# Six modulation chunks of the scan stage: products summed over row blocks on VectorE

## The chip, the core and the metric

The kernel runs on one core of one Trainium2 chip. The metric is the device time of one execution in microseconds; three runs of the kernel before gave 2157.26, 2160.35 and 2162.36 us, with a median of 2160.35 us. TensorE (PE) multiplies matrices into PSUM, VectorE (DVE) and ScalarE (ACT) work on vectors, GpSimd (POOL) does elementwise work and issues some DMAs, SyncE (SP) issues the other DMAs from one queue, in order. Each engine takes its instructions in a fixed order, and a wait at the head of an engine holds what stands behind it.

## The reference

Two layers of a diffusion trunk on 512 latent tokens and 256 context tokens of width 1024. Layer 0 mixes by a bidirectional state-space scan, layer 1 by neighbourhood attention, and both end with an MLP. Every layer is modulated by a linear map of the conditioning vectors:

```
c_act, c_ctx_act = silu(c), silu(c_ctx)
m_lat = split(c_act     @ mod_w[i] + mod_b[i], 6)   # per layer i: shift, scale, gate, twice
m_ctx = split(c_ctx_act @ mod_w[i] + mod_b[i], 6)
h = rmsnorm(x, g[0]) * (1 + m[1]) + m[0]
proj = h @ w_in                                     # then the scan, chunks of 128 tokens
scores = (C_i . B_j) * exp(cum_i - cum_j) * dt_j
y = scores @ x + exp(cum) * (C @ state)
```

The product with `mod_w` (1024 rows, 6144 columns for a layer) has only two vectors on its other side, so it is a matter of reading weights.

## The kernel before

Activations stand with channels on the partitions and tokens on the free axis. Every weight block of 128x1024 is loaded by SyncE (`wload`), split by ScalarE into a high part `wh` (L118) and by VectorE into the rest `wl` (L119), and multiplied in three products (`mm3`, L143).

The state-space stage is a loop over four groups `g`. A group has eight units (`conv_unit`): each projects one block of 128 channels (48 products of 512 or 256 columns in L143), convolves it over three tokens (one pass of ScalarE in L611, four on VectorE in L613 and L614) and passes it through silu. Groups 2 and 3 have four gate units (`z_unit`) in their middle, and eight more follow. `scan(g, ...)` is a generator; the scan of a group is stepped, `step(1)` behind pairs of products of a unit, while the units of the next group run. So scan and projection share every engine. Of a scan, VectorE makes: a mask product G (L645), and for each of 12 halves of chunks the minimum of E with cum (L713), the product of E with G (L718) and the sum of both directions (L719); then the state parts (L674 to L678), the products eb (L764) and the sum into y (L766). GpSimd weighs tokens (L662) and adds the terms (L768). TensorE multiplies E (L746), the states (L762) and the weighted tokens (L667), and needs the finished E for the first of these.

Between units one step of a further generator runs, `pieces`: the modulation of layer 0, chunks 4 to 9, each a block of 1024x512 weights loaded in four quarters `mraw` of 128x1024. One quarter holds four row blocks of 256 columns. The load of the next quarter is put into a list (`later`), which a unit issues behind its fourth pair of rows (`flush`). There is one buffer for `mraw`.

`mod_pieces` makes the products on TensorE: for each row block, 32 columns of `cact` (the two conditioning vectors stand in the first two of them) against 256 columns of weights, four row blocks in four column groups of the array (`mod_unit`, L169). `mod_finish` copies the result on ScalarE (L184), transposes it four times (L186), and VectorE sums the four row blocks (L190) and adds the bias (L191). `mod_sums`, which the MLP of layer 0 uses already, does the weighted sum over the row blocks first, then a sum over partitions with ones (L251), one copy (L255), two transposes (L257) and the bias (L262).

The order on each engine is set by a scheduler from the order in the code, the dependences and its own durations; `tc.high_priority()` moves a few instructions ahead.

Of the kernel before, what the change touches and what calls it, by code (L numbers as in the profile page):

```python
# [50 lines left out]
def trunk(ctx: ExitStack, tc: tile.TileContext, a, out, dbg=None, stop=None):  # L51
    nc = tc.nc
    pe, act, dve, pool, sp = nc.tensor, nc.scalar, nc.vector, nc.gpsimd, nc.sync
# [25 lines left out]
    def sps(tag="s"):  # L79
        return psums[tag].tile([P, 512], F32, tag=tag, name=tag)  # L80
# [83 lines left out]
    def mod_unit(ps, q, raw):  # L164


        hf, kg = divmod(q, 2)
        for j in range(4):
            mm = pe.matmul(ps[32 * j:32 * j + 32, hf * 256:hf * 256 + 256], lhsT=cact[:, 8 * kg + 2 * j:8 * kg + 2 * j + 32],  # L169
                      rhs=raw[:, j * 256:j * 256 + 256], start=kg == 0, stop=kg == 1)  # L170
        return mm.ins

    def mod_finish(l, ch, ps, cp, row_pool=None):

        for hf in range(2):
            if row_pool:
                row = row_pool.tile([P, 256], F32, tag="row", name="row", bufs=2)
            else:
                row = small.tile([P, 256], F32, tag="rt", name="row", bufs=1)
            if row_pool:  # L180
                with tc.high_priority():
                    dve.tensor_copy(row, ps[:, hf * 256:(hf + 1) * 256])
            else:
                act.activation(row, ps[:, hf * 256:(hf + 1) * 256], AF.Copy)  # L184
            for b in range(2):
                pe.transpose(cp[:, (2 * hf + b) * P:(2 * hf + b + 1) * P], row[:, b * P:(b + 1) * P], ident)  # L186
        bias = mb[:, l, ch * 4:(ch + 1) * 4].unsqueeze(2).broadcast_to([P, 4, 2])
        mt = small.tile([P, 4, 2], F32, tag="modt", name="modt", bufs=2)
        with tc.high_priority():
            dve.tensor_reduce(mt, cp.rearrange("p (b j s) -> p b s j", b=4, j=4)[:, :, 0:2], AX.X, ALU.add)  # L190
            dve.tensor_tensor(modc[:, l, ch * 4:(ch + 1) * 4, :], mt, bias, ALU.add)  # L191
# [7 lines left out]
    def mod_pieces(chunks, pool_, later=None):  # L199

        def load(l, ch, q):
            raw = pool_.tile([P, 1024], F32, tag="mraw", name="mraw", bufs=1)
            if later is None:
                sp.dma_start(raw, a["modw"][l, ch, q])
            else:
                later.append((raw, a["modw"][l, ch, q]))
            return raw

        todo = [(l, ch, q) for l, ch in chunks for q in range(4)]
        raw = load(*todo[0])  # L210
        yield
        for i, (l, ch, q) in enumerate(todo):
            if q == 0:
                ps = sps()
            mod_unit(ps, q, raw)
            if i + 1 < len(todo):
                raw = load(*todo[i + 1])
            if q == 3:
                mod_finish(l, ch, ps, sps())
            yield  # L220

    def mod_sums(chunks, pool_):

        def load(l, ch, q):
            raw = pool_.tile([P, 1024], F32, tag="mraw", name="mraw", bufs=1)
            sp.dma_start(raw, a["modw"][l, ch, q])
            return raw

        todo = [(l, ch, q) for l, ch in chunks for q in range(4)]
        raw = load(*todo[0])  # L230
        yield
        for i, (l, ch, q) in enumerate(todo):
            hf, kg = divmod(q, 2)
            if kg == 0:
                ms = pool_.tile([P, 2, 256], F32, tag="msum", name="msum", bufs=1)
            for j in range(4):
                for s in range(2):
                    c = cact[:, 8 * kg + 2 * j + s:8 * kg + 2 * j + s + 1]
                    w, t = raw[:, j * 256:(j + 1) * 256], ms[:, s]
                    if kg == 0 and j == 0:  # L240
                        act.activation(t, w, AF.Copy, scale=c)
                    else:
                        dve.scalar_tensor_tensor(t, w, c, t, ALU.mult, ALU.add)
            if i + 1 < len(todo):
                raw = load(*todo[i + 1])
            if q == 1:
                ps = sps()
            if kg == 1:
                for s in range(2):
                    j = 2 * hf + s  # L250
                    pe.matmul(ps[32 * j:32 * j + 32, :256], lhsT=ones[:, :32], rhs=ms[:, s], start=True, stop=True)  # L251
            if q == 3:
                cp = sps()
                row = small.tile([P, 256], F32, tag="rt", name="row", bufs=1)
                act.activation(row, ps[:, :256], AF.Copy)  # L255
                for b in range(2):
                    pe.transpose(cp[:, b * P:(b + 1) * P], row[:, b * P:(b + 1) * P], ident)  # L257
                bias = mb[:, l, ch * 4:(ch + 1) * 4].rearrange("p (h b) -> p h b", h=2)
                to = modc[:, l, ch * 4:(ch + 1) * 4, :].rearrange("p (h b) s -> p h b s", h=2)
                got = cp[:, :256].rearrange("p (b h s r) -> p h b s r", b=2, h=2, s=2)  # L260
                for h in range(2):
                    dve.tensor_tensor(to[:, h], got[:, h, :, :, 0], bias[:, h].unsqueeze(2).broadcast_to([P, 2, 2]), ALU.add)  # L262
            yield
# [172 lines left out]
    with tc.tile_pool(name="p0", bufs=1) as p0:  # L436
# [6 lines left out]
        for ch in (0, 2, 1, 3):  # L443
            for pr in range(2):
                raw = p0.tile([P, 2, 1024], F32, tag="raw0", name="raw0", bufs=8)
# [58 lines left out]
    ssd = sstack.enter_context(tc.tile_pool(name="ssd", bufs=1))  # L504
# [82 lines left out]
    later = []  # L587
# [219 lines left out]
            if pending is not None and next(pending, 0) == 0:  # L807
                pending = None

    pieces = mod_pieces([(0, ch) for ch in range(4, 10)], ssd, later)  # L810
    nz = 0
    for g in range(GROUPS):
        B, C, X = [None] * 2, [None] * 2, [None] * 4
# [597 lines left out]
```

## Time and profile before

| | before |
|---|---|
| median of three runs | 2160.35 us |
| profiled execution | 2166.39 us, span 2164.6 us |
| TensorE busy | 2060.4 us (95%) |
| VectorE busy | 1379.0 us (64%) |
| ScalarE busy | 1022.6 us (47%) |
| GpSimd busy | 445.1 us (21%) |
| mean granted clock of TensorE | 0.978 |

The shares are means over stages. The stage of the change goes from about 55 us to 376 us: the first load of a quarter is issued at 54.9 us, the last at 359.5 us. A busy TensorE is not TensorE at its peak, since the ends of its records are modelled; costs are read here from the start of one group of products to the start of the next. Line numbers are those of the kernel before; in the changed kernel those behind L226 are 3 higher.

### The profile page before, as it was taken

The numbers are of one execution on the slowest core, as the hardware profiler recorded it, in microseconds if no ns is written. First come the engines' busy times: TensorE is split into PE (matmuls) and PEld (weight loads), VectorE is DVE, ScalarE is ACT, GpSimd is POOL, SyncE is SP. The second block draws the span as 40 slices with busy tenths as digits, with TensorE's granted clock in tenths as the row PEclk, the third lists the DMA queues.
The fourth block names the chain that finished last, engine by engine and source line by source line (L and its number), as shares of the span: only waits on it lengthen the run. The fifth ranks groups of instructions, "written<-read, shape, count | busy, mean of one in ns | idle before, by whom it ended". The sixth has DMA issues, their size and how long they took to land.

```text
span 2164.6 us, 32307 instructions
## 1 busy us (share of the span) xinstructions
PE 2060.4 (95%) x12588; PEld 1731.3 (80%) x12588; DVE 1379.0 (64%) x2351; ACT 1022.6 (47%) x1781; POOL 445.1 (21%) x438
## 2 busy tenths in 40 slices
PE   6999998999999899999999999889999889999996
PEld 3787876878878767888888888678898768889896
DVE  5657967577683778657667244488777774345355
ACT  4575756567472644323223123456556643323244
POOL 0005435146361340000000002513222230000002
PEclk8999999999999899999999999999999999999998
DMA  6456748357575522333333121321111124222233
GB/s 256 129 162 184 242 148 240 119 165 219 194 223 178 207 78 78 114 128 119 120 114 117 59 67 60 108 79 50 57 54 54 50 80 135 90 96 89 97 108 117
DMA packets 93868, 269.70 MB, mean 125 GB/s; under 512 B 13074, under 2 KB 21652, under 8 KB 93716
## 3 DMA queue, kind: packets, MB, share of 16 engines
q1 hardware_dynamic: 85268, 242.47, 34.1%
q0 software_dynamic: 8448, 25.18, 4.4%
q8 instruction: 99, 1.62, 0.3%
q14 instruction: 53, 0.43, 0.1%
HBM read 244.27 MB, written 23.33 MB: 124 GB/s over the span
## 4 chain that ended last, share of the span: by engine, by line
PE 62%; DVE 7%; ACT 3%; DMA 2%; issue 1%; POOL 1%; SPq 0%; DVEq 0%; ACTq 0%; POOLq 0%
PE acc L943 21%; PE acc L995 20%; PE acc L143 8%; PE a L1090 4%; PE a L1101 2%; PE yp L1176 1%; DVE wl L119 1%; PE pt L1161 1%; ACT wh L118 1%; DVE xa L398 1%; PE s L251 1%; DVE ya L397 1%; PE sc L1146 1%; PE sc L1147 1%; PE s L306 0%
## 5 line engine op out<-in xcount | busy, mean ns | idle before, releaser
L118 ACT ACTIVATE wh<-raw 128x1024 fp32r<-128x1024 f32 (+1 forms) x241 | 254.3, 1056 | 648.5 <-PE acc L995 225.8
L119 DVE TENSOR_TENSOR wl<-raw,wh 128x1024 fp32r<-128x1024 f32 (+1 forms) x241 | 298.0, 1237 | 212.0 <-ACT wh L118 208.5
L143 PE MATMUL acc<-hh,wh 128*128 128x512 f32 (+1 forms) x976 | 288.1, 372 | 6.6 <-ACT wh L118 2.6
L143 PE MATMUL acc<-hl,wh 128*128 128x512 f32 (+1 forms) x976 | 266.3, 348 | 0.5 <-DVE hl L800 0.5
L143 PE MATMUL acc<-hh,wl 128*128 128x512 f32 (+1 forms) x976 | 264.7, 347 | 2.0 <-DVE wl L119 2.0
L995 PE MATMUL acc<-ah,wh 128*128 128x512 f32 (+1 forms) x832 | 246.7, 346 | 4.5 <-DVE ya L1001 4.4
L943 PE MATMUL acc<-hh,wh 128*128 128x258 f32 (+2 forms) x1024 | 240.7, 315 | 5.9 <-ACT hh L415 5.2
L995 PE MATMUL acc<-ah,wl 128*128 128x512 f32 (+1 forms) x832 | 245.0, 345 | 0.8 <-DVE wl L119 0.8
L995 PE MATMUL acc<-al,wh 128*128 128x512 f32 (+1 forms) x832 | 244.9, 344 | 0.0
L943 PE MATMUL acc<-hl,wh 128*128 128x258 f32 (+2 forms) x1024 | 239.8, 313 | 1.0 <-DVE hl L416 0.9
L943 PE MATMUL acc<-hh,wl 128*128 128x258 f32 (+2 forms) x1024 | 240.5, 313 | 0.1
L143 PEld LDWEIGHTS acc<-hh,wh 128*128 128x128 f32 (+1 forms) x976 | 156.3, 191 | 60.2 <-issue 38.1
L943 PEld LDWEIGHTS acc<-hh,wh 128*128 128x128 f32 x1024 | 160.6, 191 | 25.3 <-issue 6.6
L143 PEld LDWEIGHTS acc<-hh,wl 128*128 128x128 f32 (+1 forms) x976 | 155.2, 192 | 27.7 <-DVE wl L119 2.5
L143 PEld LDWEIGHTS acc<-hl,wh 128*128 128x128 f32 (+1 forms) x976 | 155.8, 192 | 25.2 <-issue 1.0
L943 PEld LDWEIGHTS acc<-hh,wl 128*128 128x128 f32 x1024 | 161.3, 191 | 14.0 <-issue 1.6
L943 PEld LDWEIGHTS acc<-hl,wh 128*128 128x128 f32 x1024 | 160.2, 190 | 14.4 <-DVE hl L416 2.4
L352 POOL TENSOR_TENSOR syy<-syy,last 128x512 f32<-128x512 f32 (+2 forms) x24 | 39.3, 1638 | 613.5 <-ACT last L342 613.5
L995 PEld LDWEIGHTS acc<-ah,wh 128*128 128x128 f32 x832 | 139.4, 189 | 29.8 <-issue 8.6
L995 PEld LDWEIGHTS acc<-ah,wl 128*128 128x128 f32 x832 | 139.6, 189 | 22.5 <-issue 1.2
L995 PEld LDWEIGHTS acc<-al,wh 128*128 128x128 f32 x832 | 139.7, 189 | 20.6 <-issue 0.4
L1001 DVE TENSOR_TENSOR ya<-ya,acc 128x768 f32<-128x768 f32 (+2 forms) x56 | 40.6, 726 | 163.5 <-PE acc L995 163.3
(327 smaller groups left out, 3849.5 us busy)
## 6 DMA issues: line engine op xcount, KB each, us to landing
raw<-in_w_dram SPq DMA_DIRECT2D x136, 512.0 KB, 3.3
mraw<-in_modw_dram SPq DMA_DIRECT2D x72, 512.0 KB, 3.4
raw<-in_win_dram SPq DMA_DIRECT2D x48, 512.0 KB, 4.5
E<-crow SPq DMA_DIRECT2D x96, 256.0 KB, 5.0
eb<-erow POOLq DMA_DIRECT2D x96, 128.0 KB, 5.5
raw<-in_wout_dram SPq DMA_DIRECT2D x24, 512.0 KB, 3.5
raw<-in_modw_dram SPq DMA_DIRECT2D x8, 1024.0 KB, 17.3
raw<-in_wqk_dram SPq DMA_DIRECT2D x16, 512.0 KB, 3.3
```

Of the source, the lines that this page charges most:

```text
L118: act.activation(wh[:, :n], raw[:, :n], AF.Copy)
L119: dve.tensor_tensor(wl[:, :n], raw[:, :n], wh[:, :n].bitcast(F32), ALU.subtract)
L143: mm = pe.matmul(acc[:m, s0:s1], lhsT=ww[:, i * m:(i + 1) * m], rhs=xx[:, k, s0:s1], start=first and i == 0 and j == 0, stop=last and i == ...
L251: pe.matmul(ps[32 * j:32 * j + 32, :256], lhsT=ones[:, :32], rhs=ms[:, s], start=True, stop=True)
L352: (dve if i == 1 and s1 - s0 == 256 else pool).tensor_tensor(t[:, s0:s1], t[:, s0:s1], d, ALU.add)
L397: dve.tensor_tensor(y[:, k, sl], y[:, k, sl], R, ALU.mult)
L398: dve.tensor_tensor(x[:, k, sl], x[:, k, sl], y[:, k, sl], ALU.add)
L943: pe.matmul(acc[:, d0:d0 + s1 - s0], lhsT=ww[wi], rhs=xx[:, k, s0:s1], start=k == 0 and j == 0, stop=k == KB - 1 and j == 2)
L995: pe.matmul(acc[:, s0:s1], lhsT=ww[:, k * P:(k + 1) * P], rhs=xx[:, s0:s1], start=k == 0 and j == 0, stop=k == KB - 1 and j == 2)
L1001: dve.tensor_tensor(y, y, acc[:, p0:p1], ALU.add)
L1090: pe.matmul(acc[:, :s1 - s0], lhsT=ws[ww][:, k * P:(k + 1) * P], rhs=xx[:, k, s0:s1], start=k == 0 and j == 0, stop=k == KB - 1 and j == 2)
L1101: pe.matmul(acc, lhsT=xx[:, k, i * P:(i + 1) * P], rhs=w[ww][:, sl], start=k == 0 and n == 0, stop=k == KB - 1 and n == 2)
```

## The change

The six chunks that run beside the state-space stage are made by `mod_sums` in place of `mod_pieces`. For that `mod_sums` learns to put its loads into the list `later`.

```
-    def mod_sums(chunks, pool_):
+    def mod_sums(chunks, pool_, later=None):
 
         def load(l, ch, q):
             raw = pool_.tile([P, 1024], F32, tag="mraw", name="mraw", bufs=1)
-            sp.dma_start(raw, a["modw"][l, ch, q])
+            if later is None:
+                sp.dma_start(raw, a["modw"][l, ch, q])
+            else:
+                later.append((raw, a["modw"][l, ch, q]))
             return raw
...
-    pieces = mod_pieces([(0, ch) for ch in range(4, 10)], ssd, later)
+    pieces = mod_sums([(0, ch) for ch in range(4, 10)], ssd, later)
```

What `mod_sums` does with a quarter (unchanged by the diff):

```
            for j in range(4):
                for s in range(2):
                    c = cact[:, 8 * kg + 2 * j + s:8 * kg + 2 * j + s + 1]
                    w, t = raw[:, j * 256:(j + 1) * 256], ms[:, s]
                    if kg == 0 and j == 0:
                        act.activation(t, w, AF.Copy, scale=c)
                    else:
                        dve.scalar_tensor_tensor(t, w, c, t, ALU.mult, ALU.add)
```

So a chunk has 28 such instructions on VectorE and 4 on ScalarE, and on TensorE 4 sums with ones in place of 16 products, and 2 transposes in place of 4.

VectorE in the scan of group 0, around the weight split for the unit that follows the first X block (L613, L614 and, 3 higher, L616, L617 are the convolution; sf the forward state). Before:

```order
L718 TENSOR_TENSOR E<-E,G 128x1024
L614 SCALAR_TENSOR_TENSOR xT<-acc,cols,xT 128x511
L613 SCALAR_TENSOR_TENSOR xT<-acc,cols,xT 128x255
L719 TENSOR_TENSOR E<-E 128x512
L614 SCALAR_TENSOR_TENSOR xT<-acc,cols,xT 128x255
L713 TENSOR_TENSOR E<-E,cum 128x1024
L764 TENSOR_TENSOR eb<-eb,s 128x512 x2
L766 TENSOR_TENSOR y<-y,s 128x512
L677 TENSOR_TENSOR sf<-sf,dec 128x512
L713 TENSOR_TENSOR E<-E,cum 128x1024
L678 TENSOR_TENSOR sf<-sf,s 128x512
L119 TENSOR_TENSOR wl<-raw,wh 128x1024
```

The same place on VectorE with the change (E's minimum is L716, its product L721, its sum L722 there):

```order
L722 TENSOR_TENSOR E<-E 128x512
L617 SCALAR_TENSOR_TENSOR xT<-acc,cols,xT 128x511
L616 SCALAR_TENSOR_TENSOR xT<-acc,cols,xT 128x255
L246 SCALAR_TENSOR_TENSOR msum<-mraw,cact,msum 128x256
L617 SCALAR_TENSOR_TENSOR xT<-acc,cols,xT 128x255
L246 SCALAR_TENSOR_TENSOR msum<-mraw,cact,msum 128x256
L119 TENSOR_TENSOR wl<-raw,wh 128x1024
L246 SCALAR_TENSOR_TENSOR msum<-mraw,cact,msum 128x256 x6
L716 TENSOR_TENSOR E<-E,cum 128x1024 x2
L265 TENSOR_TENSOR modc<-s,cols 128x4 x2
L769 TENSOR_TENSOR y<-y,s 128x512
L680 TENSOR_TENSOR sf<-sf,dec 128x512
```

Eight additions of one quarter stand around the weight split, and two minima, a sum into y and the state step of the scan now stand behind them.

TensorE at the end of the third chunk, in the same scan. Before, with two transposes at a time and products with E between them:

```order
L143 MATMUL acc<-hl,wh 128x512
L186 MATMUL s<-consts,row 128x128 x2
L746 MATMUL s<-E,xtok 64x128 x4
L143 MATMUL acc<-hl,wh 128x256
L143 MATMUL acc<-hh,wl 128x512
L186 MATMUL s<-consts,row 128x128 x2
L143 MATMUL acc<-hh,wl 128x256
```

With the change (ones-products are L254, transposes L260, products with E L749):

```order
L254 MATMUL s<-msum,ones 32x256
L143 MATMUL acc<-hl,wh 128x256
L143 MATMUL acc<-hh,wl 128x512
L254 MATMUL s<-msum,ones 32x256
L143 MATMUL acc<-hh,wl 128x256
L143 MATMUL acc<-hh,wh 128x512
L143 MATMUL acc<-hh,wh 128x256
L143 MATMUL acc<-hl,wh 128x512
L260 MATMUL s<-consts,row 128x128 x2
L749 MATMUL s<-E,xtok 64x128 x8
```

The products with ones depend on VectorE's additions; four projection products behind the second of them come the transposes, which depend on ScalarE's copy, and then eight products with E.

## Rows read from the trace of the kernel before

**Rows 1.** Busy us and instructions of each engine by stretch, clock, DMA share, GB/s.
```profile
core 0: us, PE busy (x) PEld busy (x) DVE busy (x) ACT busy (x) POOL busy (x), PEclk, DMA share, GB/s
55.00:193.70 138.70, 136.17 (x822) 107.83 (x820) 85.74 (x138) 78.19 (x125) 21.34 (x25) 0.99 0.47 142
193.70:264.60 70.90, 67.84 (x466) 54.98 (x465) 65.12 (x82) 50.26 (x105) 40.16 (x42) 1.00 0.82 247
264.60:300.40 35.80, 35.21 (x210) 27.06 (x209) 20.98 (x31) 19.10 (x32) 8.16 (x7) 1.00 0.34 113
300.40:376.40 76.00, 70.34 (x447) 54.08 (x445) 59.73 (x64) 50.70 (x104) 42.33 (x43) 0.96 0.80 239
```

**Rows 2.** Waits from 55 to 380: waiter, releaser, us in total, times, longest.
```profile
DVE E L713 <- DMA E<-crow: 23.0, 12, 9.0
...
PE s L746 <- DVE E L719: 3.9, 4, 1.4
PE s L186 <- ACT row L184: 3.5, 2, 2.9
...
PE s L667 <- DVE y L766: 3.1, 1, 3.1
```

**Rows 3.** TensorE's timeline, old modulation products and transposes: start, us, instructions.
```profile
207.03 0.64 PE L169 MATMUL s<-mraw,cact 128*32 128x256 f32 x8
207.60 0.62 PE L143 MATMUL acc<-hh,wh 128*128 128x512 f32 x2
...
213.20 0.38 PE L186 MATMUL s<-consts,row 128*128 128x128 f32 x2
213.34 0.36 PE L143 MATMUL acc<-hh,wl 128*128 128x256 f32 x1
```

**Rows 4.** TensorE's timeline in the MLP, sums with ones, a pair and one alone.
```profile
858.42 0.77 PE L251 MATMUL s<-msum,ones 128*32 128x256 f32 x4
859.12 0.38 PE L943 MATMUL acc<-hh,wl 128*128 128x258 f32 x1
...
876.23 0.62 PE L251 MATMUL s<-msum,ones 128*32 128x256 f32 x2
876.78 0.39 PE L943 MATMUL acc<-hh,wl 128*128 128x258 f32 x1
```

**Rows 5.** VectorE's timeline in the MLP, three scaled additions and what follows.
```profile
863.72 1.27 DVE L243 SCALAR_TENSOR_TENSOR msum<-mraw,cact,msum 128x256 f32<-128x256 f32 x3
864.91 0.95 DVE L981 TENSOR_TENSOR al<-last,ah 128x768 fp32r<-128x768 f32 x1
```

**Rows 6.** Groups of ScalarE in the MLP: count, busy us, mean ns, idle before.
```profile
L241 ACT ACTIVATE msum<-mraw,cact 128x256 f32<-128x256 f32 x40 | 18.3, 499 | 11.9 <-DMA mraw<-in_modw_dram 11.8
```

**Rows 7.** VectorE's timeline at the end of the first scan, work ahead.
```profile
244.33 7.80 DVE L713 TENSOR_TENSOR E<-E,cum 128x1024 f32<-128x1024 f32 x4
...
256.26 1.23 DVE L718 TENSOR_TENSOR E<-E,G 128x1024 f32<-128x1024 f32 x1
257.52 0.69 DVE L719 TENSOR_TENSOR E<-E 128x512 f32<-128x512 f32 x1
```

**Rows 8.** Three lines of VectorE, 150 to 380: ns min/median/max, first and last start.
```profile
L718 DVE TENSOR_TENSOR E<-E,G x21: 1210/1224/2353, 151.5 to 368.3; 128x1024 f32<-128x1024 f32 x21
...
L719 DVE TENSOR_TENSOR E<-E x23: 677/685/1532, 150.0 to 371.0; 128x512 f32<-128x512 f32 x23
...
L764 DVE TENSOR_TENSOR eb<-eb,s x18: 674/680/689, 185.8 to 366.5; 128x512 f32<-128x512 f32 x18
```

**Rows 9.** VectorE's group of E's product in the first scan, 193.7 to 264.6.
```profile
L718 DVE TENSOR_TENSOR E<-E,G 128x1024 f32<-128x1024 f32 x9 | 12.3, 1364 | 1.3 <-ACT E L717 1.2
```

**Rows 10.** TensorE's timeline, a product of the scan that waited for PSUM.
```profile
336.68 2.04 PE L667 MATMUL s<-xw,btok 128*128 128x512 f32 x2 [3.10 <-DVE y L766]
```

**Rows 11.** The two stretches around this wait, columns as in rows 1.
```profile
335.00:340.00 5.00, 3.32 (x7) 2.12 (x8) 4.11 (x5) 3.76 (x11) 3.00 (x2) 0.57 0.62 203
340.00:345.00 5.00, 5.00 (x28) 3.89 (x27) 5.00 (x6) 0.00 (x0) 4.64 (x3) 0.75 0.28 97
```

## The prediction

> **What bounds the kernel now.** I read the slices of the page first, then sums of the stretch that the change touches, then the waits inside it, and last the timelines of TensorE and VectorE. In the stretches of the state-space stage [rows 1] TensorE is busy nearly all the time: 67.84 of 70.9 us between 193.7 and 264.6, where the scan of group 0 runs beside the projections of group 1, and 70.34 of 76.0 us between 300.4 and 376.4, where the scan of group 1 runs beside those of group 2. VectorE stands close behind it there: 65.12 of 70.9 us and 59.73 of 76.0 us. Before the first scan (55 to 193.7) it is busy for 85.74 of 138.7 us, and between the two scans (264.6 to 300.4) for 20.98 of 35.8 us. So TensorE bounds the stage as a whole, and in the scans VectorE is the second limit, with 5.8 and 16.3 us to spare. What TensorE waits for [rows 2] is small and of two kinds: E, which VectorE ends (3.9 us), and the end of a modulation chunk (3.5 us for the copy on ScalarE), and once, for 3.1 us, a PSUM tile that VectorE still had to read.
>
> **The change part by part.** It concerns six chunks of modulation, each of four loads: 24 steps, from about 55 us to 376 us.
>
> Removed on TensorE: 24 product steps. Such a step (four products of 32 columns, side by side in the array) runs from 207.03 to 207.60 [rows 3], so 0.57 us, 13.7 us in all. Six of twelve pairs of transposes go, 0.14 us each by the next two rows of the same group, 0.8 us.
>
> Added on TensorE: 12 pairs of sums with ones. The pair costs 0.70 us where its two stand together and 0.55 us for each where other work stands between them [rows 4]. In the changed order 5 pairs stand together and 7 apart: 3.5 + 7.7 = 11.2 us. TensorE is left with 13.7 + 0.8 - 11.2 = 3.3 us less work. The gain is small because the old products already shared the array four at a time.
>
> Added on VectorE: 28 scaled additions of 128x256 for a chunk, 168 in all. In the later stage that already works this way three of them take from 863.72 to 864.91 [rows 5], 0.397 us each, so 66.7 us. Their number by place, counted in the changed order between the same weight splits: 70 before 193.7, 34 in the first scan, 23 between the scans, 33 in the second, 8 after. The small reductions and additions at the end of a chunk, on both sides under half a microsecond each, are left out.
>
> Added on ScalarE: 24 scaled copies at 499 ns [rows 6], 12.0 us, less six row copies. It is idle for 20 us or more in each scan [rows 1], so I take nothing; without that cover it would be 2.5 us for each scan (five copies).
>
> What of the 66.7 us is hidden:
> - Before 193.7: 70 x 0.397 = 27.8 us into 53 us of idle time. Hidden but for delays of the softplus chain; 0 to 4 us, taken as 0.
> - First scan: 34 x 0.397 = 13.5 us into 5.8 us. In the old order VectorE works ahead here for the next scan [rows 7]: four minima in 7.80 us, and two products with their sums of 1.23 + 0.69 us. In the new order one minimum (1.95 us) and these two pairs (3.8 us) come after the stretch, so 5.8 us leave it. Work is 65.1 + 13.5 - 5.8 = 72.8 us in a stretch of 70.9. With no idle time left at all that is +1.9; with all of the old idle time still there (it comes from waits in order, not from lack of work), 72.8 + 5.8 = 78.6, +7.7. I take +5, since the idle time of before was nearly all spent on waits that stay.
> - Between the scans: 23 x 0.397 = 9.1 us and the 5.8 us put off make 14.9 us, against 14.8 us idle. 0 to 6 us, taken as +2.
> - Second scan: 33 x 0.397 = 13.1 us into 16.3 us idle. Over the whole stage VectorE's wait for E to land is 23.0 us [rows 2]; part of the 16.3 us is such waits, behind which an addition can stand only if the fixed order has one there. 0 (all fit) to 13.1 (none); taken as +3.
> - After 376.4: 8 additions, VectorE idle for longer than that, nothing.
>
> New waits: TensorE now waits for the sums of VectorE before the ones-products, and for one row copy before the transposes; in the third chunk the 8 products with E of the scan stand right behind these transposes. Half as many row copies speaks for less than the old 3.5 us, the lagging sums for more; from -3.5 (gone) to +6 (each of 12 pairs waits half a microsecond), taken as 0. The load of the next quarter waits for the last addition instead of the last product, and behind it in SyncE's queue stand the loads of weights and of E. The reload is one per unit of some 12 us or more; 0 to 3 us, taken as 0.
>
> Beside GpSimd: E's sum on VectorE, which reads SBUF alone, takes 685 ns in the median and up to 1532; an addition of the same size that reads one operand from PSUM never takes over 689 in the same stretch [rows 8]. GpSimd is busy for 40.16 and 42.33 us of the two scans [rows 1]. The added operations read SBUF alone too. E's product, of four times the size of an added operation, has a median of 1224 ns over both scans and a mean of 1364 in the first [rows 8, 9], so 0.14 us on the average goes to this. For a quarter of the size I take 0.04 us for each of the 67 additions in the scans, +2.7 us; the bounds are 0 and 0.85 us (1532 less 685) for each one that meets GpSimd. The Trainium skill, page SBUF — State Buffer, section "SBUF: two separate sides", says that VectorE with two SBUF inputs and GpSimd take one port pair by an exclusive lock, and the loser waits for the whole instruction; the spread in rows 8 agrees with that, and it speaks against moving this work to VectorE.
>
> Clock: after the 3.1 us wait of TensorE before 336.68 [rows 10] the granted clock is 0.57 and 0.75 in the two slices of 5 us around and behind it [rows 11], a mixture of the two levels of 1.2 and 2.4 GHz; that costs 5 x 0.43 + 5 x 0.25 = 3.4 us at most, part of it the wait itself. One such dip more, or longer ones: 0 to 7 us, taken as +1.6 (half a dip).
>
> Sum: -3.3 + 0 + 5 + 2 + 3 + 0 + 2.7 + 1.6 = **+11 us** on the profiled execution (2166.4 us, span 2164.6), that is 2177.4. The median of the runs is 2160.35, 6.0 below the profiled one, so **2171 us** is forecast for the median.
>
> **Rivals.**
> - Faster: the additions fit into VectorE's idle time, and what goes is felt. The place is the end of the chunks: TensorE's 3.3 us, the 3.5 us for row copies, the 3.1 us wait for PSUM (the modulation tile of the changed code is held over two steps of four, not all four) and its dip of 2 us: -12, about 2149 us. For it: 53 + 5.8 + 14.8 + 16.3 = 90 us of idle time lie between 55 and 376.4 [rows 1] for 66.7. Against it: 34 additions fall where 5.8 us are idle. It decides if VectorE can put off its work ahead without TensorE noticing.
> - No change: the two scans cost 3 us more and TensorE's 3.3 us pay for it: 2160 us. For it: the 72.8 us of the first scan are only 1.9 above its length.
> - Much slower: each added operation that meets GpSimd waits for it. 67 additions x 0.56 (GpSimd's share, rows 1) x 0.85 us = 32 us, half of it on the path: +16 on the forecast, 2187 us. The lock named above would give this result. For it: 1532 against 689. Against it: most of E's sums stay at the median of 685.
>
> That the change doesn't do what it says is excluded by the order: the 24 steps are there as additions, and only 12 pairs of ones-products.
>
> **How the numbers follow.** Forecast (+4 to +20 us) 0.42; faster 0.22; no change 0.22; much slower 0.14. A difference of 0.2%, 4.3 us, is about what a measurement of this kernel tells from none. Slower by more than that: 0.42 + 0.14 less the 0.02 of the forecast's edge, 0.54; within it 0.24; faster 0.22. Signs are mixed: the forecast's own range is 2164 to 2180. The range for 8 in 10 reaches from 2148 (the faster rival) to 2191 (just past the much slower one).
>
> **What would show it.** Right: VectorE busy for over 95% of both scans, some 67 us more of it in all; TensorE's wait for E's sum well over 3.9 us, new waits for the modulation sums, and a lower clock between 200 and 400 us; the stage's end (the last projection) about 11 us later, and nothing changed behind it. Wrong: the stage's end earlier, TensorE's waits in it under 10 us, or E's sums that reach TensorE no later; then the idle time of VectorE was usable after all. If the additions' mean is far above 0.48 us, the port's rival is at work.

## The result, and the profile after

The changed kernel takes 2174.40 us (median of 5 runs, 2169.70 to 2183.57), the kernel before beside it 2162.11 us (5 runs, 2157.26 to 2165.01). The ratio is 1.0063, with a 95% interval from 1.0042 to 1.0083: slower by 13.6 us (9.1 to 18.0), where +11 us and 2171 us had been forecast. The profiled execution has a span of 2172.6 us, 8.0 more than before: the execution of before that was profiled (2166.39 us) is 4.3 us above its median, that of after (2174.40 us) is at its median, so a part of the difference does not show between the two traces.

| | before | after |
|---|---|---|
| TensorE busy | 2060.4 us | 2054.8 us |
| VectorE busy | 1379.0 us | 1443.9 us |
| ScalarE busy | 1022.6 us | 1045.0 us |
| GpSimd busy | 445.1 us | 445.5 us |
| mean granted clock of TensorE | 0.978 | 0.978 |

TensorE has 5.6 us less to do, VectorE 64.9 us more, and the time is longer: TensorE must wait more. Where it does is read from the start of the same weight split (`wl`, L119) in both traces:

| split before which | before, us | after, us | lag | lag without additions |
|---|---|---|---|---|
| the chunks begin | 59.30 | 56.96 | -2.3 | -0.3 |
| the first scan | 193.67 | 196.10 | +2.4 | -2.6 |
| the first scan has ended | 264.63 | 276.72 | +12.1 | -1.6 |
| the second scan | 300.36 | 314.36 | +14.0 | -3.4 |
| the second scan has ended | 376.45 | 382.52 | +6.1 | -8.5 |
| the later projections | 479.63 | 486.76 | +7.1 | -10.1 |

(The last column is a run told below, in which the additions are left out.) Each column is one execution, and a split stands in VectorE's order, which differs between the kernels, so a single row can be off by some us; in the run e12 below, the lag goes from -6.5 to +6.1 us between the split of 252.05 and the next. The stretches of rows 1 in the trace of after, columns as there:

```profile
55.00:193.70 138.70, 128.92 (x718) 102.16 (x716) 112.59 (x205) 80.48 (x125) 19.48 (x21) 0.98 0.45 136
193.70:264.60 70.90, 64.76 (x399) 51.84 (x398) 66.35 (x98) 45.22 (x87) 33.99 (x39) 0.95 0.78 213
264.60:300.40 35.80, 32.28 (x178) 26.09 (x178) 28.48 (x52) 28.87 (x56) 11.07 (x13) 0.95 0.50 164
300.40:376.40 76.00, 71.07 (x427) 55.42 (x426) 73.28 (x101) 47.41 (x89) 38.12 (x34) 0.98 0.74 214
```

Against [rows 1] VectorE is busy for 66.35 and 73.28 us of the two scans (94% and 96%), and TensorE is busy for 7.2 us less before the first scan and for 3.1 us less in it, a part of which is the work that went. The waits of TensorE from 50 to 395 us, columns as in rows 2:

```profile
PE s L254 <- DVE msum L246: 9.7, 4, 6.5
PE acc L143 <- DVE xT L617: 7.8, 3, 3.6
PE s L749 <- DVE E L722: 5.2, 4, 2.6
```

Of [rows 2], the wait for E has grown from 3.9 to 5.2 us, and the waits for the row copy (3.5) and for PSUM (3.1) are gone. Gone, too, is a wait at the end of a chunk that the prediction's reading left out:

```profile
PE acc L143 <- DVE modc L191: 2.2, 1, 2.2
```

All of TensorE's waits in this stretch add up to 13.0 us before and 24.9 us after. In the place of those that are gone stand two that were not there: 9.7 us for the modulation sums, and 7.8 us for the convolution (L617), which has nothing to do with modulation.

How the convolution comes into it is seen at the end of the first scan. VectorE's timeline of after (start, us, instructions, in brackets the idle time and what ended it):

```profile
258.32 1.67 DVE L246 SCALAR_TENSOR_TENSOR msum<-mraw,cact,msum 128x256 f32<-128x256 f32 x4
...
264.15 0.48 DVE L616 SCALAR_TENSOR_TENSOR xT<-acc,cols,xT 128x255 f32<-128x255 f32 x1
270.62 0.48 DVE L246 SCALAR_TENSOR_TENSOR msum<-mraw,cact,msum 128x256 f32<-128x256 f32 x1 [5.99 <-ACT msum L244]
271.02 0.48 DVE L617 SCALAR_TENSOR_TENSOR xT<-acc,cols,xT 128x255 f32<-128x255 f32 x1
```

The queue of SyncE in the same stretch, with the load of the next quarter:

```profile
260.02 0.33 SPq L594 DMA_DIRECT2D mraw<-in_modw_dram  x1
```

ScalarE there, whose scaled copy begins the next sum:

```profile
270.08 0.91 ACT L244 ACTIVATE msum<-mraw,cact 128x256 f32<-128x256 f32 x2 [7.20 <-DMA mraw<-in_modw_dram]
```

And TensorE's projection products:

```profile
268.52 0.52 PE L143 MATMUL acc<-hl,wh 128*128 128x512 f32 x2
268.88 0.51 PE L143 MATMUL acc<-hh,wl 128*128 128x512 f32 x2
271.64 0.79 PE L143 MATMUL acc<-hh,wh 128*128 128x512 f32 x2 [2.26 <-DVE xT L617]
272.24 0.84 PE L143 MATMUL acc<-hl,wh 128*128 128x512 f32 x2
...
275.37 0.50 PE L143 MATMUL acc<-hh,wh 128*128 128x512 f32 x2
```

The last four additions of a quarter run from 258.32 to 259.9. Only then is its one buffer free, and the next load goes out at 260.02 and lands 10 us later. ScalarE's copy waits 7.20 us for it, VectorE's next addition stands behind that copy at the head of VectorE for 5.99 us, and behind this addition stands the last instruction of a convolution, which TensorE needs to reuse its accumulator: 2.26 us of waiting. After it the rows of two products come every 0.57 to 0.64 us, where they came every 0.36 before the wait, until 275.37: the six of them take 3.73 us in place of 2.1. So the 2.26 us wait costs 3.9 us.

The other two waits for the convolution, 1.94 us before 220.36 and 3.58 us before 244.64, have no load in them. VectorE works ahead of them, from 211.8 to 220.2 without a pause and from 230.4 to 244.6 with one of 0.66 us, and the convolution stands behind scan products, additions and the weight split:

```profile
241.83 1.23 DVE L119 TENSOR_TENSOR wl<-raw,wh 128x1024 fp32r<-128x1024 f32 x1 [0.66 <-ACT wh L118]
242.97 1.22 DVE L721 TENSOR_TENSOR E<-E,G 128x1024 f32<-128x1024 f32 x1
244.11 0.48 DVE L617 SCALAR_TENSOR_TENSOR xT<-acc,cols,xT 128x255 f32<-128x255 f32 x1
```

```profile
244.64 1.01 PE L143 MATMUL acc<-hh,wh 128*128 128x512 f32 x2 [3.58 <-DVE xT L617]
```

Behind them, too, the products come slower: six pairs take 3.72 us from 220.36 on and five take 3.35 us from 244.64 on, each 1.6 us more than at 0.35 us a pair. With the waits that makes 3.5 and 5.2 us, so of the 12.6 us that the convolution's waits cost in the first scan 8.7 come where VectorE is at work all the time, and not from a reload.

The clock of these stretches, columns as in rows 1 (the last but two is the granted clock, a mixture of 2.4 and 1.2 GHz):

```profile
115.00:120.00 5.00, 2.62 (x6) 0.87 (x6) 4.99 (x9) 3.81 (x4) 0.00 (x0) 0.50 0.26 75
120.00:125.00 5.00, 5.00 (x25) 4.06 (x24) 1.73 (x4) 3.65 (x6) 0.00 (x0) 0.83 0.18 47
...
220.00:225.00 5.00, 4.64 (x17) 4.03 (x18) 5.00 (x10) 3.11 (x4) 2.13 (x4) 0.66 0.76 199
245.00:250.00 5.00, 5.00 (x25) 4.01 (x25) 5.00 (x10) 4.75 (x10) 0.22 (x1) 0.70 0.93 300
270.00:275.00 5.00, 3.35 (x11) 2.89 (x12) 4.38 (x11) 4.88 (x8) 0.00 (x0) 0.69 0.60 171
355.00:360.00 5.00, 3.66 (x18) 3.03 (x19) 5.00 (x7) 1.72 (x5) 4.05 (x7) 0.72 0.68 167
```

Each lies behind a wait of TensorE of 1.9 to 6.5 us, the first two behind the longest:

```profile
117.38 1.06 PE L254 MATMUL s<-msum,ones 128*32 128x256 f32 x2 [6.48 <-DVE msum L246]
```

VectorE's head waited for the DMA of E shortly before, but this is not what made the sums late. The quarter itself came later: its first addition begins when its load lands.

```profile
109.85 1.22 DVE L716 TENSOR_TENSOR E<-E,cum 128x1024 f32<-128x1024 f32 x1 [6.29 <-DMA E<-crow]
113.03 0.48 DVE L246 SCALAR_TENSOR_TENSOR msum<-mraw,cact,msum 128x256 f32<-128x256 f32 x1 [0.16 <-DMA mraw<-in_modw_dram]
```

The chain of work that ended last (start, us, what) goes through this load:

```profile
102.48 10.45 DMA mraw<-in_modw_dram
...
113.03 0.48 DVE msum L246
...
115.35 1.99 DVE msum L246 x5
117.34 0.04 issue
117.38 1.06 PE s L254 x2
```

The load goes out at 102.48, when the last addition of the quarter before, begun at 101.94, has ended, and lands 10.45 us later. So the longest wait of TensorE and the hole at 264 to 270 us have one cause, the reload behind the last addition.

The kernel before had such dips too, at other places: of [rows 10, 11], the wait before 336.68 and its clock are gone, and both slices of rows 11 have a clock of 1.00 after.

### The profile page after: what moved, and what is told of

It is laid out like the page before. It is cut to its first block, busy times and chain, and to the rows that moved or that the text cites. A ratio compares the mean times of both kernels' runs of the same rounds, so it can differ in the third digit from the quotient of the medians.

```text
span 2172.6 us, 32207 instructions
## 1 busy us (share of the span) xinstructions
PE 2054.8 (95%) x12432; PEld 1727.1 (79%) x12432; DVE 1443.9 (66%) x2519; ACT 1045.0 (48%) x1811; POOL 445.5 (21%) x438
## 4 chain that ended last, share of the span: by engine, by line
PE 78%; DVE 10%; ACT 4%; DMA 4%; issue 3%; POOL 1%; SPq 0%; DVEq 0%; ACTq 0%; POOLq 0%
PE acc L946 21%; PE acc L998 20%; PE acc L143 19%; PE a L1093 4%; PE a L1104 2%; DVE wl L119 1%; PE yp L1179 1%; DMA mraw<-in_modw_dram 1%; PE s L670 1%; PE s L765 1%; PE pt L1164 1%; ACT wh L118 1%; PE s L254 1%; PE s L749 1%; DVE msum L246 1%
## 5 line engine op out<-in xcount | busy, mean ns | idle before, releaser
L119 DVE TENSOR_TENSOR wl<-raw,wh 128x1024 fp32r<-128x1024 f32 (+1 forms) x241 | 297.6, 1235 | 175.9 <-ACT wh L118 170.4
L143 PE MATMUL acc<-hh,wh 128*128 128x512 f32 (+1 forms) x976 | 283.7, 366 | 12.6 <-DVE xT L617 9.9
L246 DVE SCALAR_TENSOR_TENSOR msum<-mraw,cact,msum 128x256 f32<-128x256 f32 x448 | 196.2, 496 | 37.0 <-DMA mraw<-in_modw_dram 24.1
```

What stands on the lines that cost most here:

```text
L119: dve.tensor_tensor(wl[:, :n], raw[:, :n], wh[:, :n].bitcast(F32), ALU.subtract)
L143: mm = pe.matmul(acc[:m, s0:s1], lhsT=ww[:, i * m:(i + 1) * m], rhs=xx[:, k, s0:s1], start=first and i == 0 and j == 0, stop=last and i == ...
```

## Experiments

Twelve kernels ran, each in 5 rounds beside the kernel before (its median was 2163 to 2166 us). Differences in us are the ratio less 1, times 2162; a run's own time less 2162 is another number, since the kernel before beside it took longer than 2162. In each run the scheduler lays the order on all engines anew, and no run holds the rest of the order fixed, so a difference of a few us can also be that of the order.

| run | ratio to before [95%] | us |
|---|---|---|
| the changed kernel | 1.0063 [1.0042, 1.0083] | +13.6 |
| e1 free additions beside old products | 1.0000 [0.9985, 1.0015] | 0 |
| e2 changed, no additions | 0.9965 [0.9949, 0.9982] | -7.6 |
| e3 changed, ones-products later | 1.0063 [1.0038, 1.0087] | +13.6 |
| e4 changed, two half buffers | 1.0032 [1.0018, 1.0047] | +6.9 |
| e5 pinned additions beside old products | 1.0037 [1.0024, 1.0051] | +8.0 |
| e6 as e5, two half buffers | 1.0042 [1.0024, 1.0059] | +9.1 |
| e7 changed, only where no scan is pending | 1.0024 [1.0010, 1.0038] | +5.2 |
| e8 old products at the places of e7 | 1.0011 [0.9997, 1.0025] | +2.4 |
| e9 changed, sums unread | 1.0022 [1.0008, 1.0036] | +4.8 |
| e10 as e5, buffer not held | 1.0038 [1.0026, 1.0051] | +8.2 |
| e11 first two chunks alone | 1.0007 [0.9993, 1.0021] | +1.5 |
| e12 last four chunks alone | 1.0023 [1.0010, 1.0037] | +5.0 |

Two theories stood at first. Theory 1: VectorE has too little time in the scans, and the additions push its other work back. Theory 2: it is the new waits, TensorE's for the sums and SyncE's for the buffer of the quarter. Later expectations call the first A and divide the second into B (the sums) and C (the buffer).

**e1, additions that nobody waits for.** The kernel before, and 168 additions from a resident tile beside its products:

```
             mod_unit(ps, q, raw)
+            for n in range(8 if q % 2 else 6):
+                t = idle[:, n % 2]
+                dve.scalar_tensor_tensor(t, tri, cact[:, n:n + 1], t, ALU.mult, ALU.add)
```

> The kernel before, with the products on TensorE as they were, and VectorE given the 168 additions of the change in the same 24 steps, on a resident constant and a tile that nobody reads. Theory 1 (the price is VectorE's work in the scans, which puts off the sums of E): about as slow as the changed kernel, +10 to +14 us on before, ratio 1.005 or more. Theory 2 (the price is waits in the fixed order: TensorE for the modulation sums, SyncE for the buffer of the quarter): 0 to +4 us, since nothing waits for these additions.

No difference, and it tells less than was meant: bound to nothing, only 20 of the additions stood in the first scan and 10 in the second, against 34 and 33 with the change. VectorE's time as such, 67 us of it, costs nothing that shows within 3 us where the scheduler may choose the place.

**e2, no additions.** The changed kernel with the additions left out; copies and ones-products stay.

```
-                        dve.scalar_tensor_tensor(t, w, c, t, ALU.mult, ALU.add)
+                        if later is None:
+                            dve.scalar_tensor_tensor(t, w, c, t, ALU.mult, ALU.add)
```

> The changed kernel without the 168 additions (its modulation sums hold the first row block only): the ones-products wait for ScalarE's copies alone. What TensorE and PSUM gain by the change, without its price: theory 1 and theory 2 both expect a time under before, by 3 us (less work of TensorE) to 12 us (with the waits at the ends of chunks and for PSUM gone), ratio 0.994 to 0.999. Not below before would mean that the change has no gain at all to set against its price.

2157.61 us, 7.6 below before by the ratio: without the additions the change is a gain, and the additions take back 21 us. Not all of the gain need be TensorE's: with the additions gone, only ScalarE's copies hold the buffer of a quarter, and every second quarter is read by nothing. By the last column of the lag table most of the gain comes after 300 us. What the additions cost is the difference of the two lag columns: 7 us up to the first scan (from -2.0 to +5.0), 8.7 in the first scan, 3.7 between, -2.8 in the second scan and 2.6 behind it, 19 us in these two executions.

**e3, ones-products later.** They are issued behind the fourth pair of rows of the next unit.

```
             if kg == 1:
-                for s in range(2):
-                    ...
-                    pe.matmul(ps[32 * j:32 * j + 32, :256], lhsT=ones[:, :32], rhs=ms[:, s], start=True, stop=True)
+                later.append(partial(finish, l, ch, q, ms))
```

> The changed kernel with the ones-products of a pair of quarters, and the end of a chunk, issued behind the fourth pair of rows of the next unit in place of the unit's end, some 4 to 5 us of TensorE later. Theory 2: TensorE's wait for the modulation sums (9.7 us and 11.0 us of its weight loads in the changed kernel) falls to under 5 us and the time by 5 to 9 us. Theory 1: that wait only turns into one for E; the time stays within 3 us of the changed kernel, +10 us or more on before.

2178.33 us, the same ratio as the change. Its waits of TensorE, 50 to 395 us:

```profile
PE s L242 <- DVE msum L269: 11.3, 5, 5.6
PE s L763 <- DVE E L736: 8.2, 4, 5.7
```

The wait for the sums has not gone with the later place (11.3 us), and that for E has grown to 8.2. The longest of the waits for sums, 5.6 us before 115.25, is again the reload's: the quarter's load goes out at 101.44 and takes 9.4 us to land, and its additions begin at 110.90. Half a unit more in the order does not cover that.

**e4, two half buffers.** A quarter is loaded in two halves of 512 columns, each into a buffer of its own.

```
-            raw = pool_.tile([P, 1024], F32, tag="mraw", name="mraw", bufs=1)
+            raws = [pool_.tile([P, 512], F32, tag="mraw", name="mraw", bufs=2) for _ in range(2)]
...
+                later.append((raw, a["modw"][l, ch, q][:, h * 512:h * 512 + 512]))
```

> The changed kernel with each quarter loaded as two halves into two buffers of half the size (same space): the load of a half waits for the additions of four, not eight, and the other half can be worked on meanwhile. Theory 2: SyncE's wait for the additions (70.9 us, 23 times) falls by a third or more, the hole of 6 us on VectorE at 264 to 270 shrinks, and the time falls by 2 to 6 us. Theory 1: nothing changes beyond 2 us.

2171.57 us, +6.9: about half of the loss is gone by the medians, though TensorE still waits 11.4 us for sums:

```profile
PE s L256 <- DVE msum L248: 11.4, 5, 7.2
PE s L751 <- DVE E L724: 7.4, 4, 4.8
PE acc L143 <- DVE xT L619: 3.9, 1, 3.9
```

The wait for the convolution fell from 7.8 (three times) to 3.9 us (once). But SyncE's wait for the additions, which was expected to fall by a third, has grown, from the first of these lines to the second:

```profile
SPq L594 <- DVE msum L246: 70.9, 23, 7.4
SPq L596 <- DVE msum L248: 106.8, 42, 10.1
```

The hole of 6 us on VectorE is gone (the longest of its kind there is 1.93 us), yet the lag grows by 11.0 us in the first scan, no less than with the change, with a wait of 4.8 us for E in its place; and the longest wait for sums, 7.2 us, is a load that lands 11.8 us after issue. So where the 6.7 us were won is not shown, and they have an uncertainty of about 5.4 by the two intervals. (The profiled execution is 4.1 us above the median of e4.)

**e5 and e6, pinned additions.** As e1, but each addition reads the loaded quarter:

```
-                    dve.scalar_tensor_tensor(t, tri, cact[:, n:n + 1], t, ALU.mult, ALU.add)
+                    dve.scalar_tensor_tensor(t, raw[:, n // 2 * 256:n // 2 * 256 + 256], cact[:, n:n + 1], t, ALU.mult, ALU.add)
```

> The kernel before, its products on TensorE unchanged, with the 28 additions of each chunk added on VectorE: each reads the same loaded quarter at the same step, but adds it to a tile of its own that nobody reads. So they stand where the changed kernel has them and hold the same buffer, but TensorE waits for no sum. The run without additions lay 8 us below the kernel before and the changed kernel 13 us above it in this way of counting, so the additions are worth about 21 us where they stand. Theory A (VectorE's time in these places is what is short): nearly all of the 21 us, so 2180 to 2187 us. Theory B (TensorE's wait for the sums at the end of a chunk): 2165 to 2170. Theory C (the last addition of a quarter releases the one buffer late, and the next load and the weights behind it in SyncE's queue start late): 2178 or more here too, but then the run with two half buffers must be far lower.

> As the run with pinned additions, but a quarter is loaded in two halves into two buffers of half its size, so that the first half can be loaded again while the second is still added. Theory A: no difference from the pinned run beyond 3 us. Theory B: 2165 to 2170. Theory C: the additions no longer hold the loads, so most of the loss of the pinned run goes, 2165 to 2170.

+8.0 and +9.1 us. The same instructions that were free in e1 cost 8 us when they stand in their places, with no one reading the sums. That is less than half of the 21, so A alone falls short by the medians, and B alone (no more than 2170) too. In e5 TensorE's products wait for late loads:

```profile
PE s L169 <- DMA mraw<-in_modw_dram: 11.9, 7, 4.7
```

That looked like theory C. e6, with halves, gained nothing, but it is no test of C: its waits for late loads stayed at 10.7 us. The next run takes them away.

**e10, pinned without holding the buffer.** The additions read a resident tile, and as factors eight columns copied from the quarter:

```
+                go = pool_.tile([P, 8], F32, tag="go", name="go", bufs=2)
+                act.activation(go, raw[:, :8], AF.Copy)
...
+                    dve.scalar_tensor_tensor(t, tri, go[:, n:n + 1], t, ALU.mult, ALU.add)
```

> As the run with pinned additions beside the old products, but each addition reads a resident tile and, as its factor, a column of a small copy that ScalarE makes of the loaded quarter. So the additions stay in their places (33 in the first scan, 30 in the second) and the buffer of the quarter is free as soon as products and copy are done. If the 8 us of the pinned run were VectorE's time in place, 2170 to 2176 us. If they were the buffer, held until the last addition, with TensorE waiting 11.9 us for late quarters there, 2162 to 2167.

+8.2 us, as e5. The wait for late loads went from 11.9 to 1.9 us, and others came up:

```profile
PE s L755 <- DVE eb L773: 6.7, 3, 4.9
PE s L186 <- ACT row L184: 5.2, 3, 3.1
PE s L755 <- DVE E L728: 3.1, 3, 2.4
PE s L676 <- DVE y L775: 2.3, 2, 1.8
PE s L169 <- DMA mraw<-in_modw_dram: 1.9, 2, 1.7
```

So beside the old products the held buffer is not what costs, within the 4 us that the intervals leave; the place on VectorE fits, and it shows as late scan products (eb, E, y). The 24 small copies that this run adds on ScalarE are a rival that no run excludes. Here a wait that was visible in the trace was worth nothing in the time.

**e9, unread sums.** The changed kernel, the additions in place, TensorE waiting for none of them.

```
+                        t = idle
                         dve.scalar_tensor_tensor(t, w, c, t, ALU.mult, ALU.add)
```

> The changed kernel, but the additions go to a tile that nobody reads; the ones-products take what ScalarE's copies leave (one 128x256 tile for both vectors), so the modulation of six chunks is left out. The additions stand in their places and hold the buffer of the quarter, but TensorE waits for no sum. Without additions this kernel was 7.6 us below the kernel before; the pinned additions beside the old products cost 8 us. If these two add up, and the other 13 us of the changed kernel are TensorE's wait for sums in VectorE's order, 2162 to 2168 us. If the additions cost their 21 us by their place and the held buffer alone, 2172 to 2178.

+4.8 us (1.7 to 7.8). So the chain from e2 over e9 to the change is -7.6, +12.3 (the additions in their places) and +8.9 (that TensorE waits for their sums), with an uncertainty of about 5 for each step by the intervals. The second step is of e9's own make in part: its ones-products wait 3.6 us for ScalarE's copies instead, and its products with E 4.1 us. Its longest waits:

```profile
PE s L754 <- DVE E L727: 8.3, 5, 2.6
PE s L754 <- ACT msum L247: 4.1, 1, 4.1
```

**e7 and e8, quiet places.** The steps are taken only where no scan is pending, with sums and with the old products.

```
-            next(pieces, None)
+            if pending is None:
+                next(pieces, None)
```

> The changed kernel, with the steps of the six chunks only where no scan is pending: in the first group, at the ends of the groups and beside the eight last gate units. The work is the same, only its place differs. Theory A: the additions cost nothing where VectorE is idle, and TensorE keeps its gain of 7.6 us, so 2155 to 2160 us, below both kernels. Theory B: the waits for the sums go along with the chunks, so about as the changed kernel, 2170 to 2176. Theory C: 2160 to 2168, since the loads still stand before weights in the queue.

> The kernel before, its products on TensorE, at the same quiet places as the run before this: what the place alone does. All theories: TensorE's work is that of the kernel before, so 2160 to 2168 us. If it falls as far as the run with sums in the quiet places, the place and not the method makes the difference, and the gain of 7.6 us belongs to the end of chunks inside the scans.

Neither beats the kernel before: +5.2 and +2.4 us, the second within its interval no difference. e8 is where it was expected; e7 (2169.48 us) lies between the ranges of theories C and B and speaks against A's. Up to the later projections both are ahead (the split of 479.63 starts at 459.86 and 456.34), partly since 13 of the 24 steps are still to come in e8; beside the last gate units they lose it. The stretch from 540 to 670 us, first of e7:

```profile
540.00:670.00 130.00, 117.56 (x678) 91.87 (x677) 112.67 (x157) 66.51 (x124) 51.18 (x49) 0.95 0.62 189
```

and of e8:

```profile
540.00:670.00 130.00, 125.08 (x794) 98.11 (x793) 74.61 (x89) 65.51 (x120) 50.62 (x47) 0.97 0.67 203
```

With sums TensorE is idle for 12.4 of 130 us there (7.6 of them are waits for the sums), with products for 4.9, though VectorE has 17 us to spare. The places were not as quiet as the expectation took them to be: the scan of the last group runs beside these units.

**e11 and e12, one part alone.** Chunks 4 and 5 by sums and the rest by products, and the reverse.

```
+    pieces = one_after_the_other(mod_sums([(0, ch) for ch in range(4, 6)], ssd, later), 8,
+                                 mod_pieces([(0, ch) for ch in range(6, 10)], ssd, later))
```

> Only the first two of the six chunks are made by sums, before the first scan (8 of 24 steps, 56 of 168 additions); the other four by products on TensorE, as before. If the loss arises where additions meet a scan, there is none here, and a third of the gain of 7.6 us that TensorE had without additions is left: 2159 to 2164 us. If the waits for sums cost the same at any place (2.2 us for each chunk of the changed kernel), 2166 to 2170.

> The other part alone: the first two chunks by products on TensorE, before the first scan, and chunks 6 to 9 by sums, which meet both scans. If the loss arises where additions meet a scan, and the two parts add up, the changed kernel's 13.6 us less the 1.5 of the first two chunks: 2173 to 2179 us. If each chunk cost the same, two thirds of 13.6, 9 us: 2171 to 2175. If the first two chunks delay what follows (the run with them alone was 3.8 us late at the start of the first scan), less than 9 us: below 2171.

+1.5 (-1.5 to +4.5) and +5.0 us (2.2 to 8.0). The first two chunks alone do no measurable harm in the run (2165.74 us lies between the two ranges that were expected), the last four do, and together they make 6.5 where the whole makes 13.6; the 7 us between are just outside what the intervals allow. Of the three cases only the last fits e12: by it the first two chunks, nearly harmless alone, make the later ones dearer. That is an inference from the three times, and how it would come about is open. In e12 the first scan begins 3.0 us earlier than with the change (its split at 193.05, not 196.10), but VectorE's order is another one from there on, too, no run parts the two, and the profiled execution of e12 is 6.4 us below its median.

## Why the prediction was right

The sign, and +11 against a measured +13.6 us, came out (+8.0 between the two profiled executions, for which the sum was made). The terms did so only in part, and errors of both signs cancelled, so that the sum came so near is luck. Of the signs named ahead, VectorE is busy for 94% and 96% of the scans and 64.9 us longer in all, the new waits for sums are there, and the clock falls in the first scan (0.95); the wait for E's sum grew less than was said (5.2 us), and the later projections are 7 us late in place of 11.

- **TensorE, -3.3 us.** Right in sign. The change without additions gives -7.6 (e2); the waits at the end of chunks and for PSUM, which the faster rival had named, go too: of [rows 2], the 3.5 and 3.1 us are gone.
- **Waits for the new sums, 0 (-3.5 to +6).** This term was mis-sized: 9.7 us of waiting in the trace against the 3.5 and 2.2 that went, +4.0, and +8.9 by e9 against the change. The upper bound took half a microsecond for each pair; it came as a few long waits, 6.5 us for the longest, which the reload of the quarter made.
- **Before the first scan, 0 (0 to 4).** The lag grows by 4.8 us, and by 7 against the run without additions. 53 us of idle time were no room for 27.8 us of additions, since the additions behind the longest wait had to follow their load, however idle VectorE was. In e11 such a delay (3.8 us at the start of the first scan) is given back in the second scan, and 1.5 us are left by the ratio.
- **First scan, +5 (1.9 to 7.7).** The lag grows by 9.7 us there. Direction and cause were right: VectorE is full, and two of the three waits for the convolution come from that (3.5 and 5.2 us with the slow products behind them). The third, 3.9 us, is the reload's, and without it the term would lie in its range.
- **SyncE's reload, 0 (0 to 3).** This is the step that had its size most wrong in the changed kernel: two reloads took 10.45 and 10.0 us from issue to landing, and TensorE waited 6.48 and 2.26 us behind them. They were read as one load per unit with time to spare; what was overlooked is that the first addition waits for the load on VectorE, with sums or a convolution behind it. e4 gives back 6.7 us with half buffers, but its trace does not show where. Beside products, which wait on TensorE, the held buffer makes no difference that was measured (e5 and e10).
- **Between the scans, +2.** +1.9 by the lag table.
- **Second scan, +3 (0 to 13.1).** Wrong in sign: the lag falls by 7.9 us. Against the run without additions it falls by 2.8, so nothing in these traces shows a price of the 33 additions there. The rest, 5.1 us, lies where the kernel before has the wait of [rows 10] and its clock, which are gone. That is not shown to be due to less work on TensorE: in e1, e5 and e6, with the old products, the lag falls there by 3, 6 and 7 us, too (in e10 it does not).
- **GpSimd's port, +2.7.** The mean of an addition is 521 ns, its median 479 and its longest 2424:

```profile
L246 DVE SCALAR_TENSOR_TENSOR msum<-mraw,cact,msum 128x256 f32<-128x256 f32 x168 | 79.4, 521 | 7.2 <-ACT msum L244 6.8 <-DMA mraw<-in_modw_dram 0.2
```

  That is 0.042 us for each on the average, as the 0.04 that was taken from the spread in [rows 8], and the much slower rival (0.85 us for each that meets GpSimd) did not come. In the first scan the mean is 484 ns, in the second 546. The longest one is in the pair of additions from 154.11 to 156.9, beside GpSimd's two operations of L665 from 154.19 to 156.24. The Trainium skill, page SBUF — State Buffer, section "SBUF: two separate sides", has VectorE with two SBUF inputs and GpSimd share a port pair by an exclusive lock. The longest addition agrees with that, and the mean says that it was seldom met. No run here separates the port from other causes of long additions.
- **Clock, +1.6.** The slices of 5 us below full clock lose 5 x (0.50 + 0.17 + 0.34 + 0.30 + 0.31 + 0.28) = 9.5 us for the six shown above and 0.8 in four more (0.95, 0.94, 0.98 and 0.97 from 240, 360, 110 and 275), 10.3 in all. Before lost 5 x (0.43 + 0.25) = 3.4 in [rows 11] and 5 x (0.34 + 0.34 + 0.35) = 5.2 in three more (0.66 from 120, 0.66 and 0.65 from 375 and 380), 8.6 in all. The difference, 1.7, is near the term, but not as half a dip more: the dips moved to other places, and two single executions don't tell 1.7 from 0; the mean clock over the span is 0.978 in both.

Of the rivals, "faster" was half there: the change without additions gains (e2), and the additions eat it. "No change" falls by the interval, since 9.1 us is its lower end.

What stays open: the division of the 21 us between VectorE's full order, the reload and the wait for sums has uncertainties of 5 us, no run takes the reload alone away from the changed kernel, and the chunks don't add up.

## What to carry to other kernels

Idle time of an in-order engine, added up over a stretch, is no room for more work: ask for each piece what it waits for and what stands behind it, since 67 us were free where the scheduler could put them anywhere (e1) and cost 8 to 12 us at fixed places. When work moves from the engine that reads a buffer quickly to one that reads it late, price the time from the last read to the landing of the next load: here 10.45 us of it lay ahead of TensorE's longest wait. A wait of TensorE is to be priced with the slower clock behind it: here 1.6 us on top of each of three waits of 1.9 to 3.6 us.

## What the runs showed of the hardware

- After a wait of 2.26 us, TensorE ran six pairs of products at 0.57 to 0.64 us each in place of 0.36, and then at full speed again (granted clock 0.69 in that slice, a mixture of 2.4 and 1.2 GHz).
- Two loads of the same quarter size (128x1024), issued at 260.0 and 273.6 us, took 10.0 and 3.2 us from issue to landing; a load's landing can't be priced by one number (the middle figure is the mean of the two):

```profile
DMA to landing us min/median/max: 3.2/6.6/10.0
```

- 168 scaled additions of 128x256 made no difference to the time beside old products when nothing fixed their place: 1.0000 [0.9985, 1.0015].
